# Last-layer weights of the filter network prepared for both orders beside the modulation, order 1's kept in DRAM

## The chip, the core and the metric

The kernel runs on one core of a Trainium2 chip. The metric is the device time of one execution in microseconds (us), the median of several runs. The engines are TensorE (PE, with its weight loads as PEld), VectorE (DVE), ScalarE (ACT), GpSimd (POOL) and SyncE (SP), which only issues DMAs here. Each engine works through its own queue in order and waits on semaphores for the others.

## The reference

One layer of a hybrid backbone is computed for 1024 latent tokens and 256 context tokens of width 1024, in float32. What bears on the change is the implicit filter of the long convolution. A small network maps a position to the values of two filters (order 0 and order 1), each with a forward and a backward half of 512 channels:

```python
h = jnp.sin(freq * (z @ w1 + b1))
h = jnp.sin(freq * (h @ w2 + b2))
h = (h @ w3 + b3).astype(jnp.float32).reshape(L, HY_ORDER, 2, HY_CH)
decay = jnp.exp(-t[:, None] * deltas[None, :])
h = h * decay[:, None, None, :]
...
return jnp.fft.rfft(k_full, axis=0)
```

`w3` has 64 rows and 2 x 2 x 512 columns, so each order uses 1024 of its columns. The spectra go into the long convolutions of both token sets:

```python
z = x1 * _long_conv(v, k_f[:, 0], filt_bias[0])
return x2 * _long_conv(z, k_f[:, 1], filt_bias[1])
```

Around it stand: adaLN (a modulation vector from `c` through a 1024 x 6144 matrix), RMS norm and modulation of the tokens, one input projection, neighbourhood attention in 8 heads beside the convolution, an output projection and a gated feed-forward net.

## The kernel before

The program is written out as a dataflow of tiles, and a planner orders the instructions of each engine ahead of time: it simulates the engines and takes, when one is free, the ready instruction that stands first in the program (some parts are raised with a priority). The order on each engine is then fixed. A semaphore wait that takes longer on the chip than in the simulation holds what is queued behind it.

The stages on the left of the program's order are these.

- **Front** (lines 500 to 526). `filter_hidden` computes the two sine layers of the filter network for all positions (`hs1`, `hs2`; range reduction on DVE, sine on ACT, matmuls of line 317). `adaln(1)` and `adaln(0)` stream 16 blocks of 512 KB of `w_ada` through four buffers (`wada`, line 221) past small matmuls (line 225). A buffer is free again when its matmuls are done.
- **Modulation** (lines 504 to 542). Tokens come in three groups: 512 and 512 latent, 256 context. For each 128-row tile: a square with row sum on ACT (251), a power on POOL (254), a scaling on DVE (514). Then `modulate` turns 128-column blocks on PE (267), scales them on ACT (269, 272) and splits them into a high and a low part on DVE (274, 275): `hh` and `hl`. The first projection column block is computed here too (530 to 542).
- **Projections** (lines 616 to 719, called from 737 to 757). 23 column blocks of `w_in` are loaded (606), split into high and low on ACT and POOL (121, 122), and multiplied by `hh` and `hl` in three products (116 to 118). `hy_chunk` goes on with the short convolution (638 to 646), `qkv` stores attention's inputs. Parts of the other four adaLN vectors are set in between.
- **Filters** (lines 371 to 496), called once, after the first `hy_chunk`. In the program's order they stand ahead of all other projections; the planner lets both run beside each other. For each order `o`: weights `Ws`, four latent channel blocks (`lat_filter`), one context part (`ctx_filter`). A part is: matmuls of the hidden layer with the weights (376), multiplication by the decays (439, 483; the decays are exponentials on ACT from the tables `dlt` and `nt`, 380), sum and difference on POOL (394, 395, tile `cs0`), a high and a low part (397 and 399, tiles `csh0/1` and `csl0/1`), the transform with the table `dft` (116 to 118 into `psfA`), a twiddle (417, 420), butterflies (451 to 463) and stores of the spectra (467, 489).
- **Chain** (lines 772 to 899). The convolutions themselves, in 40 phases of 5 chains on two lanes: PE matmuls of 805 and 877, much DVE work (819 to 890), loads of the spectra (840). 16 phases stand, raised in priority, ahead of the attention stage (910); the others are spread over attention's loop (1160 to 1163). The chain's tiles take the filters' memory, so it begins when the filters end.
- **Attention** from about 560 us. Its bias tables, queries, keys and values are loaded by DMAs that POOL issues (967 to 974), into memory that the projections give up.

The change touches how `Ws` comes about. The filter weights enter as `sum` and `difference` of the forward and backward columns, split into a high and a low part (`ws0` twice the high part over 128 rows, `ws1` the low part and the bias). `w3load(o)` (345 to 369) does this when an order begins: once before the first order (749, behind the latest load of `w_in` in SP's queue, line 748), and once between the orders (493). Its raw tile is the buffer `csl0` for both halves one after the other, its sum `cs0`, its rounded copy `csh0`: all three also serve the spectra. The tables `dft`, `dlt` and `nt` are loaded after the first `hy_chunk` in the program's order (742 to 747); `dlt` and `nt` wait for nothing there and were put among the first loads of SP by the planner. The `dft` table passes through a buffer `tm`, shared with the first projection block's results.

Of the kernel before, what the change touches and what calls it, by code (L numbers as in the profile page):

```python
# [19 lines left out]
P = 128  # L20
# [66 lines left out]
def _build(nc, tc, top, V, A, G, T, Q, I, O, dbg, upto):  # L87
# [251 lines left out]

    f2 = "p a b -> p (a b)"  # L340

    W3GO = ()
    XW = (1,)

    def w3load(o):

        ws = [ft([P, 2, 512], f"ws{i}", F32R) for i in range(2)]
        cs = slice(o * 1024, (o + 1) * 1024)
        raw = ft([P, 2, 2, 512], "GO") if o in W3GO else None
        for i in range(2):  # L350
            r = raw[:, i] if o in W3GO else ft([P, 2, 512], "csl0")
            s = ft([P, 2, 512], "cs0")
            Q.dma_start(out=r[0:64].rearrange(f2), in_=I["filt_w3"][0, :, cs])
            if i == 0:
                Q.dma_start(out=r[64:128].rearrange(f2), in_=I["filt_w3"][0, :, cs])
            else:
                V.memset(r[64:128], 0.0)
                for q in (64, 96):
                    Q.dma_start(out=r[q:q + 1].rearrange(f2), in_=I["filt_b3"][0:1, cs])
            G.tensor_add(s[:, 0], r[:, 0], r[:, 1])  # L360
            V.tensor_sub(s[:, 1], r[:, 0], r[:, 1])
            if i == 0:
                A.copy(ws[0], s)
            else:
                rd = ft([P, 2, 512], "csh1" if o in W3GO else "csh0", F32R)
                A.copy(rd, s)
                G.tensor_sub(ws[1], s, rd.bitcast(F32))
                A.copy(ws[1][64:96], rd[64:96].bitcast(F32))
        return ws

    def filters(hs1, hs2, Ws):
# [118 lines left out]

        for o in range(2):
            if o:
                Ws = w3load(o)
            for j in range(4):
                lat_filter(o, j)
            ctx_filter(o)
# [3 lines left out]
    with ies:  # L500
        hs1, hs2 = filter_hidden()
        for _ in adaln(1, wp, "tB", 4, True, xp):
            pass
        for gi, (s, col, tl) in enumerate(groups):
            xs = []
            for i in tl:
                src, row, _ = tiles[i]
                x = wp.tile([P, D], F32, tag="wada", name="x", bufs=4) if gi in XW else \
                    xp.tile([P, D], F32, tag="x", name="x", bufs=5)
                with tc.issue_after(wlast) if gi else ExitStack():  # L510
                    Q.dma_start(out=x, in_=src[0, row * P:(row + 1) * P])
                jk = xp.tile([P, D], mybir.dt.bfloat16, tag="jk", name="jk", bufs=1)
                rs = rms_scale(xp, x, D, jk, "x")
                V.tensor_scalar(x, x, rs, None, op0=ALU.mult)
                xs.append(x)
            if gi == 0:
                for wlast in adaln(0, wp, "p", 4, True, xp):
                    pass
                scalevec(A1, n1g, 1)

                w0 = ft([P, KC, P], "cs0")
                with tc.issue_after(wlast):
                    Q.dma_start(out=w0, in_=I["w_in"][0].rearrange("(k p) c -> p k c", p=P)[:, :, 0:P])
                w0s = ft([P, 2, KC, P], "GO", F32R)
                A.activation(w0s[:, 0], w0, AF.Copy, scale=DH ** -0.5)
                V.scalar_tensor_tensor(w0s[:, 1], w0, DH ** -0.5, w0s[:, 0].bitcast(F32), op0=ALU.mult, op1=ALU.subtract)
            cs = slice(col, col + P * len(tl))
            modulate(xp, xs, s, A1, 0, lambda k: (hh[:, k, cs], hl[:, k, cs]), ("p", "p", "p", "tB"))

            n = P * len(tl)  # L530
            ps = bk("fA")[:, :n]
            for k in range(KC):
                mm3(ps, w0s[:, 0, k], w0s[:, 1, k], hh[:, k, cs], hl[:, k, cs], k == 0, k == KC - 1)
            q0 = ft([P, 512], "tm", bufs=2)[:, :n]
            if s:
                q0 = q0.rearrange("p (u r c) -> p u r c", u=4, c=16)
                A.copy(q0, ps.rearrange("p (r u c) -> p u r c", u=4, c=16))
                dst = qd[0, :, 0:LL].rearrange("p (u r c) -> p u r c", r=16, c=16)[:, :, col // GW:col // GW + 8]
            else:
                A.copy(q0, ps)  # L540
                dst = qd[0, :, LL:LT]
            A.dma_start(out=dst, in_=q0)
# [194 lines left out]
    for j in range(4):  # L737
        for which in range(3):
            hy_chunk(which, j)
            if j + which == 0:  # L740

                t = ft([P, 512], "tm", bufs=2)
                e = "p a b -> p (a b)"
                Q.dma_start(out=t, in_=I["t_dft"].flatten().rearrange("(p x) -> p x", p=P))
                split(t, dft[0].rearrange(e), dft[1].rearrange(e))
                Q.dma_start(out=dlt, in_=I["t_delta"])
                Q.dma_start(out=nt, in_=I["t_nt"])
                with tc.issue_after(wloads[-1]):
                    Ws0 = w3load(0)
                filters(hs1, hs2, Ws0)  # L750
    for j in range(4):
        for which in range(3):
# [1069 lines left out]
```

## Time and profile before

| | |
|---|---|
| median of 3 runs | 1855.13 us (1854.43 to 1856.17) |
| profiled execution | 1859.47 us, span 1857.7 us |
| mean granted PE clock | 0.962 |
| DMA | 249.76 MB, 134 GB/s on the mean |

The profile records one execution. Times inside it count from the first instruction. "Busy" is the time in which an engine's instructions ran; time spent waiting for a memory port inside an instruction counts as busy. Rows of grouped instructions give the line in the program, the engine, the operation, the output tile and its inputs, the shape, the count, then busy us, mean ns of one, and the idle time of the engine just before them with what ended it. The chain of waits follows the work that ended last back to what released it. PE's matmuls overlap each other, so that their spacing and not their length is the rate. Stage by stage the execution goes: front 0 to 46 us, modulation 46 to 80, projections with filters 80 to about 450 and with the chain to 560, attention to about 840, then output projection and feed-forward to the end.

### The profile page before, as it was taken

Reading aid. Unit: us, or ns where it says so; the run is one execution under the profiler, and the core shown is the slowest. Engines: PE = TensorE matmul, PEld = TensorE weight load, DVE = VectorE, ACT = ScalarE, POOL = GpSimd, SP = SyncE. Lnnn points to the kernel's source line nnn. Section 1 sums busy time; section 2 is a strip of 40 time slices with the busy share of each in tenths; the row PEclk is TensorE's granted clock in tenths of the full one; section 3 lists DMA queues with packets and bytes.
Section 4 is the critical chain, followed back from the end, with each engine's and each line's share of the span. In section 5 each row is a group of like instructions: output and inputs, shape, how many; then the busy total and the mean of one; then the engine's idle time right before and its main releaser. Section 6 shows DMA issues by size and latency. Waiting matters only on the chain.

```text
span 1857.7 us, 27350 instructions
## 1 busy us (share of the span) xinstructions
PE 1723.9 (93%) x9999; PEld 1453.9 (78%) x9999; DVE 1368.3 (74%) x2166; ACT 892.5 (48%) x1852; POOL 396.3 (21%) x487
## 2 busy tenths in 40 slices
PE   5899999999994689897998899999999999999997
PEld 1688778788783355465886899999999999788786
DVE  4668957861878789873467888889777877556797
ACT  4755545533333576664555444444444444443452
POOL 2366656673018325500110000000000000000001
PEclk7999999999996799898998999999999999999999
DMA  7424354356445323514331444555222122934653
GB/s 265 146 75 142 112 168 131 110 149 211 145 137 160 102 80 102 140 44 144 119 106 65 147 157 146 172 176 165 76 68 67 56 74 96 342 120 136 205 189 130
DMA packets 202438, 249.76 MB, mean 134 GB/s; under 512 B 21922, under 2 KB 147987, under 8 KB 202049
## 3 DMA queue, kind: packets, MB, share of 16 engines
q1 hardware_dynamic: 190360, 230.75, 38.5%
q0 software_dynamic: 10240, 16.46, 3.7%
q8 instruction: 78, 1.28, 0.3%
q10 hardware_dynamic: 1705, 0.82, 0.2%
q14 instruction: 55, 0.45, 0.1%
HBM read 176.75 MB, written 71.20 MB: 133 GB/s over the span
## 4 chain that ended last, share of the span: by engine, by line
PE 54%; DVE 19%; DMA 13%; ACT 5%; issue 5%; POOL 3%; SPq 0%; DVEq 0%; ACTq 0%; POOLq 0%
PE psd L116 5%; PE psd L117 5%; PE psd L118 5%; PE psp L116 4%; PE psp L118 4%; PE psp L117 4%; DMA wt<-in_w_down_dram 3%; PE psa L116 2%; PE psa L117 2%; PE psa L118 2%; DMA tdr<-wt 2%; PE psc L118 2%; PE psc L117 2%; PE psc L116 2%; PE psb L117 1%
## 5 line engine op out<-in xcount | busy, mean ns | idle before, releaser
L116 PE MATMUL psp<-hh,wh 128*128 128x512 f32 (+1 forms) x552 | 200.7, 364 | 1.9 <-ACT wh L121 1.9
L117 PE MATMUL psp<-hl,wh 128*128 128x512 f32 (+1 forms) x552 | 199.0, 361 | 0.0
L118 PE MATMUL psp<-hh,wl 128*128 128x512 f32 (+1 forms) x552 | 199.0, 361 | 0.0
L1737 POOL TENSOR_TENSOR rs<-rs,mhalf 128x1 f32<-128x1 f32 x10 | 7.7, 775 | 816.4 <-DVE rs L1736 816.4
L116 PE MATMUL psa<-T,ws 128*128 128x256 f32 (+1 forms) x528 | 165.8, 314 | 3.8 <-ACT rows L1536 2.7
L117 PE MATMUL psa<-T,ws 128*128 128x256 f32 (+1 forms) x528 | 165.1, 313 | 0.0
L118 PE MATMUL psa<-T,ws 128*128 128x256 f32 (+1 forms) x528 | 164.6, 312 | 0.0
L116 PE MATMUL psd<-wd,gs 128*128 128x512 f32 x360 | 140.7, 392 | 3.6 <-ACT gs L121 3.6
L117 PE MATMUL psd<-wd,gs 128*128 128x512 f32 x360 | 141.0, 392 | 0.0
L118 PE MATMUL psd<-wd,gs 128*128 128x512 f32 x360 | 123.8, 391 | 2.0 <-DVE gs L122 2.0
L116 PEld LDWEIGHTS psp<-hh,wh 128*128 128x128 f32 x552 | 104.9, 190 | 23.2 <-issue 7.4
L118 PEld LDWEIGHTS psp<-hh,wl 128*128 128x128 f32 x552 | 104.6, 189 | 15.3 <-issue 1.2
L117 PEld LDWEIGHTS psp<-hl,wh 128*128 128x128 f32 x552 | 104.9, 190 | 14.0 <-issue 0.4
L116 PE MATMUL psc<-T,ws 128*128 128x384 f32 (+1 forms) x352 | 110.0, 313 | 6.0 <-ACT ws L121 6.0
L967 POOL DMA_DIRECT2D tb<-rpw x192 | 100.3, 530 | 58.0 <-DVE m L1079 24.3
L117 PE MATMUL psc<-T,ws 128*128 128x384 f32 (+1 forms) x352 | 110.1, 313 | 0.0
L118 PE MATMUL psc<-T,ws 128*128 128x384 f32 (+1 forms) x352 | 109.7, 312 | 0.0
L117 PE MATMUL psb<-T,ws 128*128 128x384 f32 (+1 forms) x352 | 109.4, 311 | 0.0
L118 PE MATMUL psb<-T,ws 128*128 128x384 f32 (+1 forms) x352 | 109.4, 311 | 0.0
L116 PE MATMUL psb<-T,ws 128*128 128x384 f32 (+1 forms) x352 | 109.2, 310 | 0.0
L116 PEld LDWEIGHTS psa<-T,ws 128*128 128x128 f32 x528 | 101.3, 192 | 5.5 <-ACT rows L1536 3.9
L117 PEld LDWEIGHTS psa<-T,ws 128*128 128x128 f32 x528 | 101.3, 192 | 0.0
(404 smaller groups left out, 4783.9 us busy)
## 6 DMA issues: line engine op xcount, KB each, us to landing
wada<-in_w_ada_dram SPq DMA_DIRECT2D x48, 512.0 KB
wr<-in_w_up_dram SPq DMA_DIRECT2D x44, 512.0 KB
gr<-gdr SPq DMA_DIRECT2D x44, 320.0 KB
wr<-in_w_in_dram SPq DMA_DIRECT2D x23, 512.0 KB
wt<-in_w_down_dram SPq DMA_DIRECT2D x44, 256.0 KB
tdr<-wt SPq DMA_DIRECT2D x44, 256.0 KB
gdr<-cv SPq DMA_DIRECT2D x22, 512.0 KB
wr<-tdr SPq DMA_DIRECT2D x20, 512.0 KB
```

Of the source, the lines that this page charges most:

```text
L116: T.matmul(out, ah, bh, start=start, stop=False, skip_group_check=True)
L117: T.matmul(out, ah, bl, start=False, stop=False, skip_group_check=True)
L118: T.matmul(out, al, bh, start=False, stop=stop, skip_group_check=True)
L967: blast[0] = G.dma_start(out=tv[:, :, a * 8:a * 8 + 64], in_=rpw[var, :, 2 * p_:2 * p_ + 2, :, d * 8:d * 8 + 64].rearrange("q h u x -> q ( ...
L1737: G.tensor_tensor(rs, rs, mhalf, op=ALU.pow)
```

## The change

`w3load` is called for both orders inside the modulation loop, in the second group, ahead of that group's `modulate`. The tables are loaded there too. All of these loads stand behind the group's last row tile in SP's queue.

```diff
             if gi == 1:
+                with tc.issue_after(xlast):
+                    t = ft([P, 512], "sd00")
+                    Q.dma_start(out=t, in_=I["t_dft"].flatten().rearrange("(p x) -> p x", p=P))
+                    split(t, dft[0].rearrange(f2), dft[1].rearrange(f2))
+                    Q.dma_start(out=dlt, in_=I["t_delta"])
+                    Q.dma_start(out=nt, in_=I["t_nt"])
+                    Ws0 = w3load(0)
+                    w3load(1)
```

The same instructions leave the place after the first `hy_chunk`, where `filters(hs1, hs2, Ws0)` stays. `w3load` itself is written anew: two raw tiles (`csl0` and `csl1`), sums and differences all on POOL and, for `ws0`, straight into the result without a cast; the rounded copy in `csh1`. For order 1 the results lie in other filter buffers and are stored to DRAM:

```diff
     def w3load(o):
...
+        raw = [ft([P, 2, 512], f"csl{i}") for i in range(2)]
+        V.memset(raw[1][64:128], 0.0)
+        for i, q in ((0, 0), (0, 64), (1, 0)):
+            Q.dma_start(out=raw[i][q:q + 64].rearrange(f2), in_=w3)
+        for q in (64, 96):
+            Q.dma_start(out=raw[1][q:q + 1].rearrange(f2), in_=I["filt_b3"][0:1, cs])
+        s = ft([P, 2, 512], "csh0")
+        ws0 = ft([P, 2, 512], "GE" if o else "ws0", F32R)
+        for r, t in zip(raw, (ws0, s)):
+            G.tensor_add(t[:, 0], r[:, 0], r[:, 1])
+            G.tensor_sub(t[:, 1], r[:, 0], r[:, 1])
+        rd = ft([P, 2, 512], "csh1", F32R)
+        A.copy(rd, s)
+        ws1 = ft([P, 2, 512], "csl0" if o else "ws1", F32R)
+        G.tensor_sub(ws1, s, rd.bitcast(F32))
+        A.copy(ws1[64:96], rd[64:96].bitcast(F32))
+        if o:
+            for i, w in enumerate((ws0, ws1)):
+                Q.dma_start(out=W3d[i], in_=w.bitcast(F32).rearrange(f2))
+        return ws0, ws1
```

Between the orders, `filters` reads them back in place of preparing them:

```diff
+    def w3again():
         ws = [ft([P, 2, 512], f"ws{i}", F32R) for i in range(2)]
...
+        for i, w in enumerate(ws):
+            Q.dma_start(out=w.bitcast(F32).rearrange(f2), in_=W3d[i])
         return ws
...
             if o:
-                Ws = w3load(o)
+                Ws = w3again()
```

Each of these two stores and two loads moves 512 KB.

More of the change, by code (lines that the diff above doesn't have):

```diff
@@ L340, in _build @@
     f2 = "p a b -> p (a b)"
-    W3GO = ()
     XW = (1,)
+    W3d = dr.tile([2, P, 1024], F32, name="W3d")
     def w3load(o):
-        ws = [ft([P, 2, 512], f"ws{i}", F32R) for i in range(2)]
[L348 to L368, printed above, removed]
@@ new lines, in w3load @@
+        cs = slice(o * 1024, (o + 1) * 1024)
+        raw = [ft([P, 2, 512], f"csl{i}") for i in range(2)]
+        w3 = I["filt_w3"][0, :, cs]
+        V.memset(raw[1][64:128], 0.0)
[5 more added lines that the diff above has]
+        ws0 = ft([P, 2, 512], "GE" if o else "ws0", F32R)
@@ L510, in _build @@
                 with tc.issue_after(wlast) if gi else ExitStack():
-                    Q.dma_start(out=x, in_=src[0, row * P:(row + 1) * P])
+                    xlast = Q.dma_start(out=x, in_=src[0, row * P:(row + 1) * P]).ins
                 jk = xp.tile([P, D], mybir.dt.bfloat16, tag="jk", name="jk", bufs=1)
@@ L526, in _build @@
                 V.scalar_tensor_tensor(w0s[:, 1], w0, DH ** -0.5, w0s[:, 0].bitcast(F32), op0=ALU.mult, op1=ALU.subtract)
+            if gi == 1:
+                with tc.issue_after(xlast):
[6 more added lines that the diff above has]
+                    w3load(1)
             cs = slice(col, col + P * len(tl))
@@ L740, in _build @@
             if j + which == 0:
[L742 to L749, printed above, removed]
                 filters(hs1, hs2, Ws0)
```

## The prediction

> **What bounds the kernel now.** I read the head of the page first, then busy time by stretches of the span, then who PE waited for inside the projections.
>
> ```profile
> span 1857.7 us, 27350 instructions
> ```
>
> The profiled execution took 1859.47 us (its span and 1.8 around it). The sum below is made against that; the median of the timed runs, 1855.13, lies 4.34 lower, and I take that distance off at the end.
>
> ```profile
> 46.00:80.00 34.00, 29.15 (x145) 20.38 (x143) 26.41 (x57) 28.32 (x47) 5.00 (x7) 0.95 0.50 157
> 80.00:100.00 20.00, 19.28 (x86) 16.18 (x87) 6.76 (x12) 8.46 (x10) 13.10 (x7) 0.85 0.29 82
> 240.00:260.00 20.00, 18.53 (x122) 15.19 (x121) 8.41 (x17) 8.17 (x20) 7.92 (x6) 1.00 0.50 144
> 440.00:560.00 120.00, 117.00 (x633) 97.00 (x632) 81.09 (x117) 44.09 (x118) 14.43 (x9) 1.00 0.50 161
> 560.00:600.00 40.00, 20.50 (x68) 14.91 (x68) 33.51 (x58) 16.33 (x56) 33.84 (x72) 0.63 0.58 153
> 600.00:840.00 240.00, 201.74 (x1186) 122.33 (x1184) 194.22 (x423) 145.71 (x472) 84.14 (x157) 0.92 0.35 99
> ```
>
> The columns are the length of the stretch, busy time of PE, PEld, DVE, ACT and POOL, granted clock, DMA share, GB/s. 46 to 80 is the modulation: no engine is full, but ACT (28.3 of 34) and DVE (26.4) hand work back and forth, and POOL is almost free. From 80 to 560 PE is full with projections, filters and the first chain phases; DVE, ACT and POOL have room. 560 to 600 is the start of attention: POOL issues DMAs (33.8 of 40), PE is half empty and DVE is full, mostly with chain work. In 600 to 840 PE (84%) and DVE (81%) share the load.
>
> ```profile
> PE pscA L877 <- DVE s L864: 2.2, 1, 2.2
> ...
> PE psfB L376 <- ACT ws L363: 1.1, 1, 1.1
> ```
>
> These are two of PE's waits between 78 and 560 (total us, times, longest), the longest of all and the one on `ws` that the change names: 1.1 us. So a faster preparation of the weights is worth little by itself there. What else it does must decide.
>
> **The change part by part.**
>
> *Tables, out of the front.* The loads of `dlt` and `nt` now stand behind the last row tile of the second group, so no decay can be computed before about 45 us. Before, the planner had put them ahead:
>
> ```profile
> 20.73 1.28 ACT L380 ACT_TABLE_LOAD   x1
> 22.03 1.57 ACT L380 ACTIVATE dec<-dlt,nt 128x128 f32<-128x128 f32 x5
> 23.50 0.55 ACT L320 ACTIVATE ws<-psfA,w 64x256 f32<-64x256 f32 x1
> 23.95 0.97 ACT L380 ACTIVATE dec<-dlt,nt 128x128 f32<-128x128 f32 x3
> 24.94 1.28 ACT L329 ACT_TABLE_LOAD   x1
> 26.24 0.63 ACT L329 ACTIVATE csh<-sd 64x512 f32<-64x512 f32 x1
> ```
>
> ```profile
> 26.92 1.96 PE L317 MATMUL psfB<-csh,w 64*64 64x512 f32 x2 [2.78 <-ACT csh L329]
> ```
>
> PE sat 2.78 us until that sine, and the adaLN matmuls that free weight buffers stand behind it in PE's queue. With one table load of 1.28 and 2.5 us of decays gone, the sine is bound by DVE's range reduction. Ends: 0 and −2.8; I take −1.5, about half, since DVE is then late next. The decays come back after the modulation, where ACT has 11.5 of 20 us idle (80 to 100): 0 there; without that cover they cost the same 2.5 and one table load. The Trainium skill's page "ScalarE: Activation LUTs", section "What ACT_TABLE_LOAD costs", puts a drain of about 1.38 us beside the load of 1.283. The rows show 1.28 and the sine 0.02 behind it, with no drain; by the page this saving could be 1.4 larger.
>
> *Weights of both orders, into the modulation.* The instructions, by their durations of before:
>
> ```profile
> L360 POOL TENSOR_TENSOR cs<-csl 128x512 f32<-128x512 f32 x2 | 3.1, 1540 | 1.3 <-DMA csl<-in_filt_b_dram 1.3
> L367 POOL TENSOR_TENSOR ws<-cs,csh 128x1024 fp32r<-128x1024 f32 x1 | 2.4, 2385 | 1.2 <-ACT csh L366 1.2
> ...
> L122 POOL TENSOR_TENSOR dft<-tm,dft 128x512 fp32r<-128x512 f32 x1 | 1.3, 1283 | 0.0
> ```
>
> ```profile
> L366 ACT CAST csh<-cs 128x1024 fp32r<-128x1024 f32 x1 | 1.1, 1054 | 0.5 <-POOL cs L360 0.5
> L363 ACT CAST ws<-cs 128x1024 fp32r<-128x1024 f32 x1 | 1.1, 1053 | 3.0 <-POOL cs L360 3.0
> L368 ACT CAST ws<-csh 32x1024 fp32r<-32x1024 f32 x1 | 1.0, 1046 | 2.5 <-POOL ws L367 2.5
> L121 ACT CAST dft<-tm 128x512 fp32r<-128x512 f32 x1 | 0.6, 614 | 0.0
> ```
>
> POOL: per order four adds or subtractions of 128x512 (1.28 undisturbed, 1.54 on the mean) and one of 128x1024 (2.39), that is 7.5; twice 15.0, and 1.3 for `dft`: 16.3 us. ACT: two casts per order (1.05 each; the L363 cast is gone), 4.2, and 0.6 for `dft`: 4.8 us. DVE: two memsets stay and two subtractions per order leave. All of it comes earlier in program order than the second and third group's modulation and so goes ahead of it. DMAs: two raw sets of three 256 KB loads, the tables, two stores and later two loads of 512 KB; SP has little else to issue there, and DMA is 50% busy.
>
> ```profile
> L275 DVE TENSOR_TENSOR hl<-mo,hh 128x512 fp32r<-128x512 f32 (+1 forms) x24 | 14.4, 601 | 3.2 <-ACT hh L272 2.7
> ...
> L269 ACT ACTIVATE mo<-psp,mods,A 128x512 f32<-128x512 f32 (+1 forms) x18 | 12.6, 705 | 3.4 <-DVE hl L275 3.2
> ```
>
> ```profile
> L399 DVE TENSOR_TENSOR csl<-cs,csh x20: 1203/1217/2487, 109.4 to 416.5; 128x1024 fp32r<-128x1024 f32 x20
> ```
>
> DVE waits there for ACT (2.7 us on L272) and ACT for DVE (3.2 us on L275): the two work in turn. ACT's idle time there is 34 − 28.3 = 5.7, enough for 4.8 only if it fell in the right places. The L399 row (shortest, median, longest ns) is a DVE subtraction of the filters that takes 1.2 us, and 2.5 at its longest, in stretches where POOL works beside it. If each POOL operation held DVE for its whole length, 16.3 − (34 − 26.4) = 8.7 us would be added; at the other end 0. I take +4.5, the middle, nearest to the 4.8 of ACT. The Trainium skill, page "GPSIMD Engine Reference", section "Specifications", says that POOL shares its SBUF interfaces with VectorE, with contention for DVE instructions that read two SBUF inputs. It speaks for the upper end; L399's longest duration agrees.
>
> *The work that leaves 80 to 100.* PE is busy 19.28 of 20 there with projections: 0.
>
> *Order 1: a read in place of a preparation.*
>
> ```profile
> 242.16 6.42 DMA csl<-in_filt_w_dram
> ...
> 251.65 0.39 PE psfB L376
> ```
>
> ```profile
> 216.26 1.67 POOL L394 TENSOR_TENSOR cs<-sd,sd 128x512 f32<-128x512 f32 x1 [3.22 <-DVE csl L399]
> ```
>
> ```profile
> 269.22 1.29 POOL L394 TENSOR_TENSOR cs<-sd,sd 128x512 f32<-128x512 f32 x1 [1.51 <-DVE sd L439]
> ```
>
> PE's direct wait of 1.1 goes, and with it most of the 1.47 that PE idles in 240 to 260: −1.5 (ends 0 and −1.5). The larger matter is the filters' own chain. The raw tiles shared `csl0` and `cs0` with the spectra, so the next order started only when the last spectrum was through: 53 us lie between the last L394 of order 0 and the first of order 1. `ws` itself is free after order 0's last weight matmul, so two reads of 512 KB can land long before. I expect the filters to lead by about 11 us from the start (weights are ready at 80, not at 97) and 25 to 30 more here. PE being full until 560, this lead saves nothing by itself.
>
> *What the lead does.* The first chain phases begin when the filters end:
>
> ```profile
> 458.09 2.59 PE pscA L805 x12
> ```
>
> What is left of those phases at 560 fills DVE until 600. Some 35 us earlier, they would be done near 560. The wait of 2.2 on L864, in the last projection, goes: −2.2 (ends 0 and −2.2). PE then does this work ahead of attention instead of in its half-empty start:
>
> ```profile
> L877 PE MATMUL pscA<-s,idft 128*128 128x256 f32 x22 | 8.8, 558 | 7.7 <-DVE s L819 3.9 <-DVE s L864 3.8
> L805 PE MATMUL pscA<-s,dftf 128*128 128x256 f32 x16 | 6.2, 574 | 9.1 <-DMA s<-lxd 9.1
> ```
>
> 38 matmuls at 2.59 / 12 = 0.216 each are 8.2 us, paid where PE is full: +8.2. In return up to 33.5 us of DVE and those matmuls leave 560 to 600, and later phases can fill that hole. If half of it, 16 us of DVE, is taken out of 600 to 840 and PE (84% busy) lets most of that through, attention ends some 13 us sooner. Net −5; ends −15 and +8.2.
>
> Sum: −1.5 + 4.5 − 1.5 − 2.2 − 5 = −5.7. 1859.47 − 5.7 = 1853.8, less 4.34: **1849.4 us**.
>
> **The rivals.** They are priced the same way, around 1855.1.
>
> *The lead buys nothing.* The planner orders the chain for attention as before, and both gain and price of the last term are missing: −0.7, 1854.4. For it: PE is full to 560 and POOL's DMAs gate attention's start. Against it: 560 to 600 shows chain work on DVE that has room before 560 (81 of 120 us busy).
>
> *The chain's matmuls are paid and not given back* (slower). The 8.2 us go into the full stretch, and attention, held by its own scores and transposes, returns nothing: −1.5 + 4.5 − 1.5 − 2.2 + 8.2 = +7.5, 1862.6. It turns slower once attention returns less than about 7.5 of the 13. For it: the full PE in 440 to 560. Against it: DVE at 81% through attention.
>
> *POOL holds the modulation's DVE* (slower). The upper end, +8.7, which also eats the first 11 us of the lead, so that nothing behind comes back: −1.5 + 8.7 − 1.5 = +5.7, 1860.8. It turns slower from a modulation that is 3.0 longer, that is from a first projection matmul (now the row below) that is 1.5 later, if nothing behind gives that back:
> ```profile
> 80.72 0.79 PE psp L116
> ```
>
> For it: L399's 2.5 us, and the scaling factors of the later tiles (L254) in the same POOL queue. Against it: most POOL operations in the filters do not stretch their neighbours (median 1.217). The page named above gives this result.
>
> *It does not do what it says.* The stores or the reads of the prepared weights stand behind a waiting SP instruction, and order 1 begins as late as before: −1.5 + 4.5 = +3.0, 1858.1.
>
> **How the numbers follow.** The forecast gets 0.54, the lead that buys nothing 0.16, the reads that come late 0.06, the chain's price 0.12, POOL's hold 0.12. About 0.2%, 3.7 us, is what a measurement of this kernel can tell from no change. Faster by more: 0.54; within: 0.16 + 0.06 = 0.22; slower: 0.12 + 0.12 = 0.24. The forecast's own range goes from 1838 (the last term near −15) to 1852. With the other cases the range is 1838 to 1864; about 0.1 stays out below and 0.1 above.
>
> **What would show it.** Right: no table load of L380 before 26 us; the first `psp` matmul between 79 and 85; the first L376 of order 1 before 225 with no wait on `ws`; first L805 near 420; less DVE time in 560 to 600. Wrong: DVE rows of the modulation (L275, mean 0.60) well over 1 us; order 1 still starting near 250; 600 to 840 as long as before in spite of the lead.

## The result, and the profile after

The changed kernel takes 1869.73 us (1866.25 to 1869.93, 4 runs) against 1855.16 of the kernel before on the same chip: ratio 1.0074, 95% interval 1.0056 to 1.0091. It is 14.6 us slower, where the prediction said 5.7 faster, and outside the range. Its profiled execution took 1866.25 us.

The head of its page, and the same stretches of the span as before (length, busy time of PE, PEld, DVE, ACT and POOL with instructions, granted clock, DMA share, GB/s):

```profile
span 1864.3 us, 27375 instructions
```

```profile
46.00:80.00 34.00, 21.67 (x84) 14.92 (x83) 26.23 (x35) 23.98 (x41) 22.00 (x18) 0.80 0.43 131
80.00:100.00 20.00, 14.15 (x79) 11.02 (x79) 19.01 (x32) 14.50 (x32) 9.15 (x6) 0.95 0.12 41
240.00:260.00 20.00, 20.00 (x130) 16.90 (x129) 11.12 (x24) 10.58 (x27) 5.22 (x4) 1.00 0.39 114
440.00:560.00 120.00, 119.60 (x657) 99.78 (x656) 102.18 (x145) 49.13 (x132) 28.87 (x28) 1.00 0.54 162
560.00:600.00 40.00, 31.34 (x170) 25.97 (x169) 21.39 (x36) 11.34 (x34) 17.60 (x40) 0.91 0.55 168
600.00:840.00 240.00, 201.10 (x1133) 118.28 (x1131) 185.99 (x400) 143.21 (x445) 103.05 (x192) 0.92 0.40 111
```

From 46 to 100 PE does 35.8 us of work where it did 48.4. DVE is as busy as before in the first row with 35 instructions in place of 57: each has become longer. Later the kernel gets back what was hoped for: the idle time in 240 to 260 is gone, 440 to 560 is fuller, the hole at 560 to 600 half filled. Three rows of its timeline and one of the chain that ended last give the places:

```profile
53.52 1.28 ACT L386 ACT_TABLE_LOAD   x1 [0.49 <-DMA nt<-in_t_nt_dram]
54.81 1.57 ACT L386 ACTIVATE dec<-dlt,nt 128x128 f32<-128x128 f32 x5
105.43 0.50 PE L116 MATMUL psp<-hh,wh 128*128 128x512 f32 x1 [0.56 <-ACT wh L121]
```

```profile
419.08 2.59 PE pscA L813 x12
```

The decays have left the front, but not for the time after the modulation. The first projection matmul comes at 105.43, where it came at 80.72. The chain starts 39 us earlier than at 458.09.

For all that follows I cut each execution into stages at PE matmuls: **front** up to the last adaLN matmul, **modulation** up to the last matmul of the first projection block (`psfA<-hh,GO`), **projections** up to the last `psp<-hh,wh`, **attention** up to the last `psX`. Lengths count from the start of one such matmul to the start of the next; the stretches shown lie about 0.2 us later. Modulation, projections and attention before, then after, as stretches:

```profile
44.40:78.70 34.30, 30.05 (x154) 20.92 (x146) 26.46 (x57) 27.71 (x45) 5.00 (x7) 0.94 0.51 165
78.70:559.90 481.20, 470.92 (x2820) 394.56 (x2820) 333.56 (x477) 219.50 (x484) 239.23 (x186) 0.99 0.45 137
559.90:877.10 317.20, 251.39 (x1431) 157.57 (x1430) 243.05 (x501) 180.03 (x554) 120.35 (x230) 0.88 0.38 107
```

```profile
40.40:102.30 61.90, 42.84 (x204) 31.54 (x196) 50.27 (x77) 42.53 (x77) 31.34 (x24) 0.84 0.39 127
102.30:584.20 481.90, 468.04 (x2800) 393.71 (x2800) 365.81 (x524) 221.15 (x510) 227.36 (x173) 0.99 0.48 146
584.20:882.20 298.00, 244.92 (x1402) 148.49 (x1401) 198.41 (x431) 163.95 (x501) 121.22 (x231) 0.90 0.36 100
```

The front is 4.0 shorter, the modulation 27.6 longer, projections and attention together 18.5 shorter, the rest 1.6 longer: +6.7, the difference of the two spans. The other 7.9 of the 14.6 us lie between these executions and their medians (before 4.3 above its own, after 3.5 below). The modulation holds 50 more PE matmuls than before; these are filter work that used to come later. The rest behind attention lies between 977.9 and 984.9 us in the 20 profiles of the table, so its 1.6 means nothing.

Stage lengths in us, one profile each (two executions of the changed kernel differ by 5.0 in the front and by up to 2.4 in the others); ratio to the kernel before, measured on the same chip (the medians come from several chips, so runs are compared by their ratios):

| run | front | modul. | proj. | att. | proj.+att. | median | ratio, 95% interval |
|---|---|---|---|---|---|---|---|
| before | 44.2 | 34.3 | 481.2 | 317.3 | 798.4 | 1855.2 | 1 |
| after | 40.2 | 61.9 | 481.9 | 298.0 | 779.9 | 1869.7 | 1.0074 (1.0056 to 1.0091) |
| after_again | 45.2 | 60.2 | 482.2 | 295.6 | 777.8 | 1869.9 | 1.0066 (1.0051 to 1.0081) |
| late_both | 47.0 | 34.0 | 488.4 | 297.4 | 785.8 | 1848.1 | 0.9955 (0.9939 to 0.9972) |
| tables_late | 40.7 | 38.4 | 467.2 | 331.5 | 798.7 | 1860.7 | 1.0019 (1.0007 to 1.0032) |
| on_dve | 40.0 | 56.0 | 488.5 | 294.8 | 783.2 | 1863.9 | 1.0041 (1.0025 to 1.0057) |
| hold_filters | 40.7 | 48.3 | 498.2 | 294.7 | 792.9 | 1867.9 | 1.0061 (1.0044 to 1.0079) |
| second_late | 45.7 | 48.8 | 487.0 | 298.3 | 785.4 | 1859.1 | 1.0003 (0.9988 to 1.0019) |
| pool_only | 43.5 | 43.9 | 486.3 | 299.0 | 785.3 | 1857.4 | 1.0004 (0.9991 to 1.0016) |
| act_only | 43.2 | 37.1 | 486.7 | 296.1 | 782.8 | 1851.8 | 0.9978 (0.9962 to 0.9993) |
| all_late | 40.8 | 34.1 | 484.2 | 304.3 | 788.5 | 1848.7 | 0.9951 (0.9936 to 0.9966) |
| lead_held | 43.2 | 34.4 | 488.7 | 297.7 | 786.4 | 1850.0 | 0.9955 (0.9941 to 0.9970) |
| lead_raw | 47.5 | 34.0 | 490.8 | 298.8 | 789.7 | 1847.7 | 0.9952 (0.9934 to 0.9971) |
| chain_held | 47.1 | 34.0 | 476.8 | 309.2 | 786.0 | 1848.9 | 0.9958 (0.9942 to 0.9974) |
| filters_end_held | 46.4 | 33.9 | 474.3 | 302.8 | 777.1 | 1836.2 | 0.9887 (0.9865 to 0.9909) |
| inplace | 46.4 | 33.9 | 466.4 | 330.0 | 796.4 | 1859.1 | 1.0009 (0.9995 to 1.0023) |
| before_chain | 44.9 | 34.0 | 479.8 | 313.5 | 793.4 | 1855.1 | 0.9989 (0.9972 to 1.0005) |
| before_end_held | 43.5 | 34.3 | 476.4 | 312.5 | 788.9 | 1854.6 | 0.9981 (0.9967 to 0.9995) |
| end_held_more | 43.8 | 33.9 | 461.7 | 348.1 | 809.9 | 1869.3 | 1.0071 (1.0049 to 1.0093) |
| after_end_held | 41.6 | 61.7 | 470.0 | 309.0 | 779.0 | 1864.4 | 1.0037 (1.0021 to 1.0054) |

### The profile page after: what moved, and what is told of

It reads as the page before. It is cut to its first block, busy times and chain, and to the rows that moved or that the text cites. A ratio compares the mean times of both kernels' runs of the same rounds, so it can differ in the third digit from the quotient of the medians.

```text
span 1864.3 us, 27375 instructions
## 1 busy us (share of the span) xinstructions
PE 1726.9 (93%) x9999; PEld 1455.3 (78%) x9999; DVE 1379.5 (74%) x2162; ACT 887.4 (48%) x1848; POOL 411.1 (22%) x491
## 4 chain that ended last, share of the span: by engine, by line
PE 49%; DVE 15%; DMA 8%; issue 4%; ACT 4%; POOL 2%; SPq 0%; DVEq 0%; POOLq 0%; ACTq 0%
PE psd L116 6%; PE psd L117 6%; PE psd L118 6%; PE psa L116 2%; DMA wt<-in_w_down_dram 2%; PE psa L117 2%; PE psa L118 2%; PE psp L116 2%; PE psp L118 2%; PE psp L117 2%; PE psc L117 2%; PE psc L118 2%; PE psc L116 2%; PE psb L117 2%; PE psb L118 2%
```

## The experiments

The theory after the result: POOL's preparation of the weights holds DVE in the modulation, and the price is larger than I took; what the new `w3load` does for the rest is worth having. The rivals: the filters' first steps, let in ahead of the third token group by weights that are ready early; ACT's additional work; the tables.

### What the modulation paid

**hold_filters** keeps the changed kernel and holds the filters back to the end of the modulation:

```diff
-                filters(hs1, hs2, Ws0)
+                with tc.issue_after(mlast):
+                    filters(hs1, hs2, Ws0)
```

(`mlast` is the last matmul of the first projection block.)

> The changed kernel with the filters placed behind the last matmul of the q0 projection, which ends the modulation; the preparation of the weights stays in the modulation. Theory F (the filters' first steps, 18 of whose weight matmuls and their sines, sums and decays run from 59.5 us on ahead of the third group's modulation, cost most of the 24.7 us): first projection at 84 to 92 us, 1850 to 1858 us. Theory H (POOL's hold of DVE by the preparation): first projection still at 98 or later, 1865 to 1870 us.

```profile
40.90:89.20 48.30, 36.39 (x155) 26.54 (x148) 36.72 (x58) 35.90 (x59) 22.35 (x18) 0.76 0.57 177
```

The modulation is 13.6 us shorter, and the time nearly the same: 1867.9. What the filters' steps took in the modulation they return behind it (projections and attention 792.9 against 779.9). Theory F had the first effect nearly right (the first projection comes at 92.6, just behind its 84 to 92) and its worth wrong: this work was only moved. What stays is 48.3 − 34.3 = 14.0 us. Who pays shows in DVE's operations in the modulation (count, busy us, mean ns); first before, then hold_filters, then the changed kernel:

```profile
L275 DVE TENSOR_TENSOR hl<-mo,hh 128x512 fp32r<-128x512 f32 x16 | 10.9, 689 | 1.6 <-ACT hh L272 1.3
L274 DVE CAST hh<-mo 128x512 fp32r<-128x512 f32 x12 | 5.0, 421 | 0.1
L514 DVE TENSOR_SCALAR x<-x,rs 128x1024 f32<-128x1024 f32 x6 | 4.5, 754 | 1.7 <-POOL rs L254 1.5
```

```profile
L275 DVE TENSOR_TENSOR hl<-mo,hh 128x512 fp32r<-128x512 f32 x16 | 14.2, 896 | 1.4 <-ACT hh L272 1.1
L274 DVE CAST hh<-mo 128x512 fp32r<-128x512 f32 x12 | 9.2, 772 | 0.4 <-ACT mo L269 0.4
L520 DVE TENSOR_SCALAR x<-x,rs 128x1024 f32<-128x1024 f32 x6 | 6.5, 1086 | 3.5 <-POOL rs L254 2.8 <-DMA csl<-in_filt_b_dram 0.6
```

```profile
L275 DVE TENSOR_TENSOR hl<-mo,hh 128x512 fp32r<-128x512 f32 x16 | 14.6, 915 | 0.2
L274 DVE CAST hh<-mo 128x512 fp32r<-128x512 f32 x12 | 10.3, 861 | 0.4 <-ACT mo L269 0.4
...
L520 DVE TENSOR_SCALAR x<-x,rs 128x1024 f32<-128x1024 f32 x6 | 6.5, 1086 | 4.1 <-POOL rs L254 4.1
```

The same instructions take 3.3 + 4.2 + 2.0 = 9.5 us more in hold_filters and 11.0 more in the changed kernel. PE pays too: its granted clock in the modulation falls from 0.94 to 0.76, and 155 matmuls take 36.4 us where 154 took 30.1. PE is idle for 12 of the 48 us there, so I take this for a consequence of the waiting; no run separates it.

**pool_only** measures that by itself, in a kernel without the preparation in the modulation (late_both, below). On a loaded tile, with a result that nobody reads:

```diff
+            if gi == 1:
+                with tc.issue_after(xlast):
...
+                    for _ in range(4):
+                        G.tensor_add(d1[:, 0], d0[:, 0], d0[:, 1])
+                        G.tensor_sub(d1[:, 1], d0[:, 0], d0[:, 1])
+                    for _ in range(2):
+                        G.tensor_sub(d1, d0, d0)
```

**act_only** has five `A.copy(d1, d0)` of 128x1024 in the same place.

> As the run with both orders prepared behind the modulation, plus ten POOL operations in the modulation, eight of 128x512 and two of 128x1024 on a loaded tile, whose result nobody reads: 15.0 us of POOL by the durations of before, no work on ACT, DVE or PE, one load of 512 KB. Theory H (POOL holds DVE): L274, L275 and L520 of the modulation take 8 to 10 us more in sum, the modulation lasts 42 to 45 us in place of 34, 1857 to 1862 us. Rival W (what cost in the modulation is ACT's and the filters' work): modulation 34 to 37 us, 1848 to 1852 us.

> The same with five ACT copies of 128x1024 in the modulation in place of the POOL operations, 5.3 us of ACT (the preparation's share there was 4.8). Theory H: modulation 34 to 37 us, 1848 to 1852 us. Rival W (ACT and DVE hand work on in turn, so that each us of ACT is paid): modulation 39 us, 1853 to 1856 us.

POOL's and DVE's rows of pool_only:

```profile
L540 POOL TENSOR_TENSOR csh<-csl 128x512 f32<-128x512 f32 x4 | 5.9, 1474 | 0.0
L539 POOL TENSOR_TENSOR csh<-csl 128x512 f32<-128x512 f32 x4 | 5.8, 1456 | 0.0
...
L542 POOL TENSOR_TENSOR csh<-csl 128x1024 f32<-128x1024 f32 x2 | 4.4, 2193 | 0.1
```

```profile
L275 DVE TENSOR_TENSOR hl<-mo,hh 128x512 fp32r<-128x512 f32 x16 | 16.4, 1043 | 0.5 <-ACT hh L272 0.2
L274 DVE CAST hh<-mo 128x512 fp32r<-128x512 f32 x12 | 9.8, 831 | 0.4 <-ACT mo L269 0.3
L520 DVE TENSOR_SCALAR x<-x,rs 128x1024 f32<-128x1024 f32 x6 | 5.5, 912 | 0.7 <-POOL rs L254 0.6
```

16.1 us of POOL work without any consumer lengthen three DVE lines by 5.5 + 4.8 + 1.0 = 11.3 us (in late_both they take 10.9, 5.0 and 4.5 as before), the modulation by 9.9 (43.9 against 34.0) and the ratio from 0.9955 to 1.0004. Theory H is shown: it needs neither filters nor ACT. act_only loads the same tile, and its three DVE lines stay at 10.9, 4.9 and 4.5 us, so the load is not the cause. Its 5.4 us of ACT cost 3.1 in the modulation and 0.0023 in the ratio, about 4 us, with intervals that overlap: between theory and rival, and not the main part.

**on_dve** moves the ten operations of the preparation from POOL to DVE (`G.tensor_add`, `G.tensor_sub` become `V.`).

> The changed kernel with the preparation's sums, differences and the last subtraction on DVE in place of POOL (ten operations). Theory H (POOL's operations hold DVE in the modulation, L275 1.5 to 1.8 us beside them where it is 0.69 else, and delay the scale factors in POOL's queue): the first projection comes back from 105.4 to 95 or less, 1856 to 1863 us. Rival W (not the hold but the work as such, and the filters' first steps that the early weights let in ahead of the third group's modulation): the first projection stays at 103 to 112, 1866 to 1876 us.

Two of its rows:

```profile
L275 DVE TENSOR_TENSOR hl<-mo,hh 128x512 fp32r<-128x512 f32 x16 | 11.2, 708 | 0.4 <-ACT hh L272 0.4
...
L274 DVE CAST hh<-mo 128x512 fp32r<-128x512 f32 x12 | 6.4, 549 | 0.0
```

The stretch is nearly gone (0.3 + 1.4 us), but DVE now does the ten operations itself, 8 x 0.69 + 2 x 1.22 = 8.0 us. The modulation is only 4 to 6 us shorter, the time 0.3% better. The first projection comes at 99.9, between theory H (95 or less) and rival W (103 or more). POOL was no free place: these operations cost DVE about as much there as on DVE.

**second_late** moves only order 1's preparation behind the modulation (`with tc.issue_after(wloads[-1]): w3load(1)`, after the first `hy_chunk`).

> The changed kernel with only the second order's preparation moved behind the modulation; order 0's and the tables stay in it. Theory H (POOL's preparation stretches DVE: 9.5 us more in L274, L275 and L520 of the modulation for two preparations and dft): DVE's stretch in those three lines about half, 4 to 6 us, first projection minus the filter matmuls ahead of it 6 to 8 us earlier, 1857 to 1863 us. Rival W (what costs is the first preparation, or the tables, whatever the second does): 1866 to 1870 us.

L275, L274 and L520 take 6.4 us more than before (12.9 + 6.3 + 7.6 against 20.4), a little over theory H's 4 to 6, the modulation 48.8 with 28 filter matmuls ahead, and the time is that of the kernel before. Order 1's half of the preparation had cost 0.6 to 0.7%; moving the rest too (late_both) brings another 0.5%.

**tables_late** is the kernel before with only the loads of `dlt` and `nt` moved behind the second group's last row tile.

> The kernel before with one edit: the loads of dlt and nt stand behind the second group's last row tile, so the decays cannot be computed in the front. In the changed kernel the adaLN matmuls ended 4.0 us earlier (44.2 us to 40.2 us). Theory A (the front's gain is from the decays that leave ACT, and the whole kernel behind moves by it): adaLN ends near 40.2, first projection near 77, 1851 us. Rival B (the gain is lost again in the modulation, where the decays are computed now, with two table loads): first projection within 1 us of 80.7, or later, 1855 to 1858 us.

```profile
40.90:79.30 38.40, 32.67 (x151) 22.99 (x146) 26.59 (x57) 31.32 (x54) 4.11 (x7) 0.88 0.47 156
```

Rival B holds. The front ends 3.5 us sooner, and the modulation lasts 4.1 longer: ACT does 9 instructions and 3.6 us more there, since the decays and their table load are put into the modulation. In time it is slightly slower, but the planner also ordered the rest otherwise (1338 projection matmuls stand ahead of the last filter matmul, where it was 1225), so the time alone shows nothing of the tables. (Over all 20 profiles the front takes 45.1 us on the mean with the decays in it and 41.9 without, each with a spread of 4 to 6 us.) **all_late**, with the tables behind the modulation too, has neither cost,

> As the run with both orders prepared behind the modulation (1848.1 us), and the loads of dlt and nt behind the projection's weight loads too, so that the decays can be computed neither in the front nor in the modulation. With the tables alone moved into the second group, the front ended 3.5 us earlier and the modulation took 4.1 us longer, 3.6 us of it more work on ACT: nothing was left. Theory (the decays only need a place where ACT has room): first projection near 77.5, 1843 to 1846 us, some 3 us less than the run without it. Rival (the filters then begin later, or the gain is taken back in attention as a front gain of 3.5 us was): 1847 to 1850 us.

and 1848.7 us: the front's gain shows in the stages and not in the time (rival).

**after_again** is the changed kernel once more.

> The changed kernel unchanged, for a second profile and a time on the same chip as the runs beside it: 1866 to 1870 us, first projection 105 +- 2 us.

It confirms the time (1869.9). Its first projection comes at 108.1, outside the 105 ± 2, as its front was 5.0 us longer than in the first profile.

### What the early preparation is worth

**late_both** keeps the new `w3load`, DRAM included, but calls it for both orders at the old place, behind the modulation:

```diff
-                    Ws0 = w3load(0)
-                    w3load(1)
...
+                with tc.issue_after(wloads[-1]):
+                    Ws0 = w3load(0)
+                    w3load(1)
                 filters(hs1, hs2, Ws0)
```

> Both orders' weights and the tables are prepared at the place of the kernel before (behind the modulation, while the projections run); order 1 still goes through DRAM. So the lead of the filters between the orders is kept (25 to 30 us) and nothing is added to the modulation. Theory A (the lead is worth something: of the 24.7 us that the changed kernel was late at its first projection, attention gave back all but 6.9, and the lead did that): first projection at 81 +- 2 us as before, attention ends 10 to 18 us earlier than before, 1838 to 1846 us. Rival B (the lead is worth nothing, attention only absorbed the late start because it was held by something that does not depend on it): same as before, 1853 to 1857 us. Rival C (the second order's preparation is itself paid where PE is full): slower than before by some 5 us, 1860 us.

0.45% faster than the kernel before and 1.2% faster than the changed one: the modulation is as before, and projections and attention are 12.6 us shorter. Attention ends 10 us earlier, as theory A wanted; the time, 0.45% less, falls short of its range. The prediction's reason would be the lead, with the chain earlier. Three runs test that.

**lead_held** lets the reads of the prepared weights wait for order 0's last spectrum (`with tc.issue_after(klast): Ws = w3again()`); **lead_raw** sends them through a tile of `csl0` and one of `cs0` as before; **chain_held** places the chain's first phases behind the 18th projection (`phases(16)` under `tc.issue_after(plast[17])`).

> As the run with both orders prepared behind the modulation, but the two reads of order 1's prepared weights are issued only behind the last product of order 0's last spectrum, so that the lead between the orders is taken away and nothing else. Theory A (the lead is what attention gives back): first filter matmul of order 1 after 235 us, first chain matmul of L812 later than 445 us, attention as long as before (over 310 us from the last projection), 1854 to 1860 us. Rival B (the gain comes from the second preparation's other place, or from what left the stretch between the orders): still 1846 to 1850 us.

> As the run with both orders prepared behind the modulation (1848 to 1849 us), but the two reads of order 1's prepared weights go one after the other through a tile of csl0, a POOL copy into cs0 and an ACT copy, so that order 1 waits for order 0's last spectra as it did in the kernel before. The last try left the reads where they were (216.5 us) and said nothing. Theory A (what attention gives back is the lead between the orders): first weight matmul of order 1 after 240 us, first chain matmul of L812 after 445 us, attention (last projection to last psX) over 310 us, 1854 to 1859 us. Rival B (the other place of the preparation, not the lead): 1847 to 1851 us.

> As the run with both orders prepared behind the modulation, but the chain's phases are placed behind the 18th of the 23 projections, so that its first matmul has 1296 projection matmuls ahead of it (1140 in the run without this, 1289 in the kernel before). Routing order 1 through the old tiles delayed its first weight matmul by 33 us and still the filters ended at 418 us as in the run without, the chain began at 430 us and attention was 299 us long; so the start of order 1 was not what attention gives back. Theory C (it is how much of the chain PE does ahead of the last projection: 128 chain matmuls in every run whose attention took 295 to 304 us, 98 before with 317 us, 52 with 331 us): about 100 chain matmuls ahead, attention 310 to 322 us, projections shorter by 5 to 9 us, 1853 to 1859 us. Rival D (the gain is in the filters' own earlier end, or in what the preparation no longer does between the orders, and not in the chain's place): 1846 to 1851 us.

lead_held is a miss: the reads were issued at 216.5, as in late_both (219.5, its front being 3.8 longer), so it says nothing. In lead_raw the first weight matmul of order 1 comes at 256.9, in place of 224.2 in late_both, and the filters still end at 417.9 (416.9): order 1 has 521 projection matmuls between its parts, where it has 676 in the kernel before. No time is lost: theory A falls as written, the start of order 1 is not it. The stretches of chain_held, after those of late_both:

```profile
81.10:569.50 488.40, 476.63 (x2850) 400.58 (x2850) 347.60 (x524) 228.09 (x522) 249.97 (x190) 0.99 0.48 145
569.50:866.90 297.40, 248.07 (x1401) 153.15 (x1400) 212.07 (x450) 167.65 (x512) 120.38 (x230) 0.88 0.38 105
```

```profile
81.30:558.00 476.70, 467.56 (x2818) 394.10 (x2818) 309.77 (x467) 215.45 (x476) 248.85 (x190) 0.99 0.47 143
558.00:867.30 309.30, 252.21 (x1434) 159.13 (x1433) 247.02 (x507) 181.56 (x559) 121.20 (x230) 0.89 0.40 110
```

32 matmuls and 35 to 38 us of DVE work go from one stage to the other, the projections get 11.7 us shorter, attention 11.9 longer: a move without gain or loss. Theory C falls as well, and with it the step of the prediction that wanted 13 us from it.

**filters_end_held** also puts the end of the filters where the kernel before has it (1226 projection matmuls ahead of the last filter matmul; 1225 before, 1068 in late_both): order 1's last latent tile and its context tile are placed behind the 11th and 13th projection.

```diff
+        if part:
+            with tc.issue_after(plast[10]):
+                lat_filter(1, 3)
+            with tc.issue_after(plast[12]):
+                ctx_filter(1)
+            return
```

> As the run with both orders prepared behind the modulation, but the last latent tile and the context tile of order 1's filters are placed behind the 11th and the 13th projection, so that the last filter matmul has 1226 projection matmuls ahead of it (1068 without this, 1225 in the kernel before) and the chain's first 1284 (before: 1289). Theory E (the filters' earlier end, which empties DVE, ACT and POOL ahead of attention, gives the 12 us): projections and attention together 796 to 800 us, 1854 to 1860 us. Rival G (the preparation between the orders cost them, or attention's order only came out another way): 783 to 790 us, 1846 to 1851 us.

1836.2 us, 1.1% faster than before and the fastest of all, where theory E wanted it as slow as before and rival G as fast as late_both: neither had it. **before_end_held** makes this edit in the kernel before; **end_held_more** holds the two tiles one projection longer; **after_end_held** makes it in the changed kernel.

> The kernel before with the last latent tile and the context tile of order 1's filters placed behind the 11th and the 13th projection (1228 projection matmuls ahead of the last filter matmul, 1225 without). Order 1's weights are still prepared between the orders. Theory L (the gain of 21 us belongs to order 1 being prepared ahead): projections and attention together 793 to 800 us, 1853 to 1859 us. Rival M (it belongs to the held tiles, which spread the filters' last work, whoever prepares the weights): 775 to 785 us, 1835 to 1845 us.

> As the fastest run (both orders prepared behind the modulation, filters' last two tiles held), with the two tiles one projection later: 1349 projection matmuls ahead of the last filter matmul (1226 there), 24 rows of chain matmuls ahead of the last projection in place of 49. Theory N (the gain has a best place, since the chain moves into attention when the filters end late): projections and attention together 780 to 800 us, 1840 to 1858 us. Rival O (the later the better): below 777 us, under 1835 us.

> The changed kernel with the same two tiles held (1228 projection matmuls ahead of the last filter matmul, 923 without). If the price of the preparation in the modulation (some 10 us for POOL, 3 for ACT, the rest given back) and the gain behind it add up: first projection near 105 as in the changed kernel, 1850 to 1858 us. If the gain behind depends on the modulation: 1862 to 1870 us.

Projections and attention of filters_end_held, then of before_end_held. The filters end and the chain begins at nearly the same places in PE's order (1226 and 1228 projection matmuls ahead of the last filter matmul, 1284 and 1286 ahead of the first of the chain):

```profile
80.50:554.80 474.30, 468.36 (x2820) 394.15 (x2820) 319.51 (x478) 221.64 (x490) 247.42 (x190) 0.99 0.47 144
554.80:857.60 302.80, 248.32 (x1431) 153.80 (x1431) 239.75 (x496) 177.11 (x544) 120.78 (x230) 0.90 0.40 112
```

```profile
78.00:554.40 476.40, 469.89 (x2820) 394.45 (x2820) 322.34 (x477) 220.55 (x484) 239.06 (x186) 0.99 0.46 139
554.40:866.90 312.50, 252.15 (x1431) 158.12 (x1429) 242.12 (x500) 178.26 (x551) 120.31 (x230) 0.89 0.38 108
```

With order 1 prepared ahead, the two stages take 11.8 us less though filters and chain stand alike, about as much as without the hold (12.6, late_both against before). 2.1 of it are in the projections, 9.7 in attention, whose matmuls are the same in number. Which wait carries it into attention I could not name; it is spread over many. A rival stays open: the order is not the same. At attention's seventh matmul before_end_held goes on with `qkv` and filters_end_held with the chain, and the orders differ from there, so part or all of the 9.7 us may come from the planner's order and not from the earlier preparation as such. The held tiles by themselves are worth 0.2% in the kernel before: its time is theory L's, its stages lie between L and M. One projection more (end_held_more) costs 33 us: 48 of the chain's 320 matmuls stand ahead of the last projection, where it was 98, and attention then takes 348 us. That is theory N's direction, beyond its range. In the changed kernel the hold helps 0.3% and does not add up: the second case of its expectation.

**inplace** calls the new `w3load(1)` between the orders, without DRAM, and **before_chain** moves the chain in the kernel before by 7 of 1656 matmuls.

> As the run with both orders prepared behind the modulation, but order 1 is prepared at its old place between the orders, by the new instructions and without DRAM. The last filter matmul then has 1331 projection matmuls ahead of it. Theory G1 (the preparation between the orders costs what was won, or the late filters do): projections and attention together 796 to 805 us, 1854 to 1862 us. Rival G2 (the new form of the preparation, or chance in the order of attention): 783 to 790 us, 1846 to 1851 us.

> The kernel before with the chain's phases placed behind the 18th projection, so that 1296 projection matmuls stand ahead of the first of them in place of 1289: a change of next to nothing in the order. Theory (the times follow from where the work stands): projections and attention together 797 to 800 us, 1854 to 1858 us. Rival K (attention's order comes out another way at the least change, and that alone moves the time by 10 us): outside 793 to 803 us.

inplace is no faster than before, so the new form of the preparation is not what helps; its place is, or what follows from it (its filters also end later, at 467 us). But it would be too much to say that preparing ahead is worth 12 us at every order: end_held_more, whose filters end there too, is 13.5 slower than inplace in these two stages. before_chain's 5.0 us less in the stages (793.4, between its theory and rival K) go with a ratio whose interval includes 1: differences of 5 us in this table are within what a small change of order does. (Attention runs in another order there, too, from its 23rd matmul on.) What is shown is this: the six kernels that prepare order 1 ahead behind the modulation, add no work to the modulation, and begin the chain earlier than the kernel before or at about the same place (1139 to 1296 projection matmuls ahead of it, 1289 before) are all 0.4 to 1.1% faster than it. Why stays open.

## Why the prediction was wrong, point by point

- **Front, −1.5.** Measured −4.0, in this pair, beyond the end of −2.8 (over the 20 profiles 3.2 on the mean). The mechanism was right. But "The decays come back after the modulation" at no cost failed: the planner puts them into it, and tables_late shows 4.1 us for it. The term comes out at nothing.
- **Preparation in the modulation, +4.5.** This step failed, where it says "I take +4.5, the middle, nearest to the 4.8 of ACT". 27.6 us were added; 13.6 are filter steps that come early and are given back (hold_filters), which the prediction did not see; 14.0 are paid. Measured one by one, the tables cost 4.1 (tables_late), POOL's hold on DVE 9.9 (pool_only) and additional ACT work of about the preparation's size 3.1 (act_only). These make 17.1, so they overlap in the 14.0, and how they share it is not shown; POOL's hold is the largest. The upper end of 8.7, POOL's time less DVE's idle time, came close to pool_only: 16.1 − (34.0 − 26.5) = 8.6 by it, 9.9 measured. I took the middle of 0 and 8.7 with nothing to support it but ACT's 4.8, and held the rival's case weak because L399's median of 1.2 us seemed to say that most operations are not held. A median does not show the held ones; the longest of that row, 2.5, did.
- **80 to 100, 0.** No run takes it alone. PE was idle for 0.7 us there, so it could not have been more.
- **Waits on order 1's weights and on L864, −1.5 and −2.2.** Both are gone. In their place PE waits for DVE's twiddles in the filters, between the first and the last projection of the changed kernel, where DVE is busy for 365.8 us in place of 333.6:

```profile
PE psfA L116 <- DVE GE L426: 9.6, 5, 3.7
PE psfA L116 <- DVE GO L426: 2.1, 3, 1.3
```

  Before, these were 0.2 and 1.6. The stage's idle PE time rose from 10.3 to 13.9 us.
- **The lead, 0, and what it does, −5.** The lead came (order 1's first weight matmul at 194.5, for "before 225"; filters end 41 us earlier; chain at 419.08 for "near 420"; less DVE work in 560 to 600). With the 13.6 us of moved filter work taken out, projections and attention gave 4.9 us where this and the last point promised 8.7. The working was wrong all the same: the chain's matmuls and their return cancel (chain_held, 11.7 against 11.9), and the gain of 12 us that comes with the preparation ahead (late_both) is not tied to them.
- **The rivals.** "POOL holds the modulation's DVE" was the right one, at 12%. Its 8.7 us were close to what pool_only measures (9.9); that the hold eats the first 11 us of lead was wrong. Its +5.7 against the pair's +6.7 is luck: it is added up from three terms of which none was measured at its size (front −4.0, modulation +27.6, projections and attention −18.5). Its 1860.8 missed, like the forecast, the 7.9 us between the profiles and the medians: 4.34 were taken off for the profile before, while the changed kernel's lay below its median. The signs that I named: "L275 well over 1 us" was badly chosen, as its mean over 16 is 0.92 while single ones take 1.76; the late first projection was the one that told.

## What to carry to other kernels

A POOL operation beside DVE work that reads and writes SBUF is not in a free place: price it at its whole length less DVE's idle time (that gave 8.6 of 9.9 us here), and look at DVE's busy time per instruction, since the wait is hidden in it. When inputs become ready earlier, a planner that takes the first ready instruction in program order will also pull their consumers ahead; ask what it will start next, and hold what should not start. And before a gain is put down to a lead, put the led work back and see whether the gain goes: here it did not.

## What the runs showed of the hardware

In these traces DVE waits for a POOL operation to its end, and an operation with a single SBUF input waits too. From the changed kernel's timeline, DVE and POOL (start, length):

```profile
58.58 1.76 DVE L275 TENSOR_TENSOR hl<-mo,hh 128x512 fp32r<-128x512 f32 x1
60.27 1.50 DVE L274 CAST hh<-mo 128x512 fp32r<-128x512 f32 x1
...
66.78 2.50 DVE L274 CAST hh<-mo 128x512 fp32r<-128x512 f32 x1
```

```profile
58.07 1.72 POOL L359 TENSOR_TENSOR csh<-csl 128x512 f32<-128x512 f32 x1
59.75 1.73 POOL L360 TENSOR_TENSOR csh<-csl 128x512 f32<-128x512 f32 x1
...
66.20 2.79 POOL L364 TENSOR_TENSOR ws<-csh,csh 128x1024 fp32r<-128x1024 f32 x1
```

They alternate: each of these DVE operations, 0.69 or 0.42 us alone, ends some 0.3 to 0.6 us after the POOL operation that began before it, and POOL's 1.28 becomes 1.72 when DVE is ahead. Operations with an operand in PSUM were not held. Two lines of the filters in the kernel before, in the same stretches beside POOL (shortest, median and longest ns):

```profile
L420 DVE SCALAR_TENSOR_TENSOR GO<-psfA,tw,tm x48: 473/736/753, 129.3 to 444.9; 128x512 f32<-128x512 f32 x32, 128x256 f32<-128x256 f32 x16
```

```profile
L452 DVE TENSOR_TENSOR GE<-GE x8: 672/684/2875, 126.0 to 398.4; 128x512 f32<-128x512 f32 x8
```

L420, from PSUM, never takes more than 0.753 us, though 28 of its 80 operations (the row shows 48, the others write `GE`) begin inside a POOL operation of over 1 us; L452, all in SBUF, takes up to 2.875. The Trainium skill, page "SBUF — State Buffer", section "Who interferes with whom", describes an exclusive lock on a port pair that POOL and DVE share, taken for a whole instruction, by DVE operations with two SBUF inputs or in a two-port mode; an operation with one SBUF input that is not in such a mode is outside it. By that rule the trace agrees for L275, L420 and L452, and for L274 and L520 if they run in such a mode, which no run here shows by itself.
